# One rule more for issuing the mixer's steps, and a new operand layout for RWKV7's chunk products, in a three-layer forward pass

## The chip, the core and the metric

The program runs on 1 core of one Trainium2 chip: TensorE (PE in the rows, PEld its weight loads), VectorE (DVE), ScalarE (ACT), GpSimd (POOL), and SyncE (SP), whose queue starts the DMAs. The metric is device microseconds per execution. Before the change three runs took 3031.47, 3031.53 and 3036.08 us, median 3031.53. One further execution was profiled; the rows below come from it.

## What is computed

512 tokens of width 2048 pass through three layers and a final norm, in float32: an attention layer with decaying scores ("fox"), a sliding-window attention layer ("swa"), and a mixer of two linear recurrences side by side ("mix"). Each layer multiplies by a large input matrix and a large output matrix. What the change touches is the RWKV7 half of the mixer: 16 heads of width 64, each with a recurrence over tokens.

```python
def _rwkv7_scan(r, w, k, v, a_vec, b_vec):
    def step(S, inp):
        r_t, w_t, k_t, v_t, a_t, b_t = inp
        sa = jnp.einsum('bhij,bhj->bhi', S, a_t)
        S = S * w_t[:, :, None, :] + sa[..., None] * b_t[:, :, None, :] + v_t[..., None] * k_t[:, :, None, :]
        return S, jnp.einsum('bhij,bhj->bhi', S, r_t)
...
o_rwkv, v_first = _rwkv7_branch(rw, v_first, ...)
o_hgrn = _hgrn2_branch(hg, lower_bounds[l], g_norm_w[l])
y = jnp.einsum('btc,cd->btd', jnp.concatenate([o_rwkv, o_hgrn], axis=-1), w_out[l])
h = _layer_norm(ALPHA * h + y, ln_w[l], ln_b[l])
```

The kernel computes the scan in 4 chunks of 128 tokens. Within a chunk it needs, per head, the 128 x 128 products of the decayed vectors (a, r) with (b, k), then the inverse of a triangular matrix built from them, then a short chain that carries the state from chunk to chunk.

## The kernel before

**The stream.** All large products go through `stream`. Weights come in chunks of 128 x 512 (`raw`), are split into a high part (`wh`, ScalarE) and a low part (`wl`, GpSimd), and each slot of the stream issues three TensorE products of 512 columns (high x high, high x low, low x high; `mm3`) into a PSUM tile `proj`. In the rows these are `proj<-hh,wh`, `proj<-hl,wh` and `proj<-hh,wl`; here they are called stream products. There are 10272 of them in the program.

**The steps.** All other work is written as threads: lists of steps, each a Python function that issues a few instructions on several engines. Before each slot `stream` calls `side`, which goes through the threads and issues every step that `ready` lets through, within a budget. `ready` decides by a planner's clock (`Clock`, `Engine.cost`): a step may go once the step before it in its thread is finished by that clock (plus a margin) and the events it needs are past. `require` and `drain` issue steps whether they are ready or not. TensorE runs its instructions in the order in which they were issued, so a step issued too early makes the stream products behind it wait too.

**PSUM.** A step that multiplies takes a PSUM tile from a pool: `s` and `t` have 2 buffers each, `y` 1, `proj` 3. A new tile can be written only when the one that had the buffer before has been read out by DVE or ACT. The planner's clock knows of this (`tile` notes when the old tile is free, and `note` lets the engine wait for it), but `ready` does not ask for it.

**RWKV7.** Eight units (pairs of heads) follow each other; unit `u` has the threads prep, M, K and B of `rwkv_unit`. The steps the prediction speaks of, with the tile names that the rows show:

- `p_lora`: products `s<-wdh,uph` and three like it into both `s` tiles, read out by ACT into `sgt` and `ez`. `p_kk2`: head sums `t<-pm,ones_r`, `t<-pr,ones_r`, read out by DVE (`pm<-t`). `p_tok`: four transposes, `t<-ident,bk` or `t<-ident,ev`, read out by ACT (`tokb`, `tokk`, `tokv`).
- `m_split`, `m_split2` and `m_step`, four times per unit (once per chunk): the operands `bk` and `ar` are split into high and low parts (`bkhl`, `arhl`), then `s<-arhl,bkhl` products into both `s` tiles, one per head, read out by four DVE operations (`kt`, `yh`). `m_zo`: `t<-tokv,kt`, read out by ACT (`zo`).
- `inv_8` and `inv_16`: many short DVE operations on `ly` that invert small blocks. `lev16` to `lev32b`, the level steps: 112 very small products (`t<-td,yh`, `t<-wd,ly`, `t<-ly,wd`).
- `ch_z`, `ch_u`, `ch_u2`, `ch_u3`, `ch_s`, `ch_o`: the chain over chunks. `ch_z` is `t<-sbd,ar`, read out by DVE into `chz`; `ch_u` and `ch_u3` are `t<-chz,wd` (or `t<-zo,wd`), read out by DVE into `chu`. `f_1` to `f_3`: group norm, DVE operations on `gn`, then transposes `t<-ident,zo`.

The other half, HGRN2, has eight units of its own (`hgrn_unit`) with tiles from the same two pools, and follows while the stream goes on. Nearly all instructions are recorded at one line (L175, a helper), so rows are told apart by tile names.

Of the kernel before, what the change touches and what calls it, by code (L numbers as in the profile page):

```python
# [6 lines left out]
F32 = mybir.dt.float32  # L7
# [22 lines left out]
class Clock:  # L30
# [7 lines left out]
    def __init__(self):  # L38
        self.t = dict.fromkeys(("tensor", "vector", "scalar", "gpsimd", "sync"), 0.0)
        self.w, self.r, self.free, self.dead = {}, {}, {}, set()  # L40
        self.fin = 0.0
        self.aset = None
        self.mode = None

        self.port = {"vector": [], "gpsimd": []}
# [11 lines left out]
    def note(self, eng, cost, outs, ins, lat=0.0, mode=None, shared=False):  # L57
# [27 lines left out]
            del p[:-24]  # L85
        self.t[eng] = t + cost
        fin = t + cost + lat
        for c, kind in use.items():
            d = self.w if kind else self.r
            if d.get(c, (0.0, eng))[0] <= fin:  # L90
                d[c] = (fin, eng)
        self.fin = max(self.fin, fin)

    def last(self, name):

        return max([v[0] for d in (self.w, self.r) for k, v in d.items() if k[0] == name] + [0.0])


def isap(x):
# [89 lines left out]
class Timed:  # L189
    def __init__(self, clock, nc):  # L190
        for n in ("tensor", "vector", "scalar", "gpsimd", "sync"):
            setattr(self, n, Engine(clock, getattr(nc, n), n))


class Kern:
# [109 lines left out]
    def set(self, ev):  # L305
        self.ev[ev] = self.clock.fin
# [29 lines left out]

    def ready(self, th):
        return th["steps"] and th["ready"] <= self.clk and all(
            self.ev.get(e, 1e9) <= self.clk for e in th["steps"][0][1])

    def side(self):
        t0 = self.clk
# [916 lines left out]
    def rwkv_unit(self, st, u):  # L1259
# [142 lines left out]
        def m_split(c):  # L1402
            def f():
                if c == 0:
                    S["zo"] = P("zo", (128, 4, 2, 128), bufs=2)
                bk = S["bk"][:, c]
                S["bkh", c] = x = P("bkhl", (128, 2, 2, 128), F32R, 2)
                S["arh", c] = y = P("arhl", (128, 3, 2, 128), F32R, 2)
                for h in range(2):
                    nc.scalar.activation(x[own[h], h], bk[own[h]], AF.Copy)  # L1410
                nc.scalar.activation(y[:, 2], S["ar"][:, c], AF.Copy)
            return f

        def m_split2(c):
            def f():
                ar, bk, x, y = S["ar"][:, c], S["bk"][:, c], S["bkh", c], S["arh", c]
                for h in range(2):
                    a, b = own[h], own[1 - h]
                    nc.scalar.activation(y[b, h], ar[a], AF.Copy)
                    nc.vector.tensor_tensor(out=x[b, h], in0=bk[a], in1=x[a, h].bitcast(F32),  # L1420
                                            op=ALU.subtract)
                    nc.vector.tensor_tensor(out=y[a, h], in0=ar[a], in1=y[a, 2].bitcast(F32),
                                            op=ALU.subtract)
            return f

        def m_step(c):
            def f():
                p = [ps("s", (128, 2, 256)) for h in range(2)]  # L1430
                x = S["bkh", c]
                y = [S["arh", c][:, i].rearrange("p a t -> p (a t)") for i in range(3)]
                for i in range(2):
                    for h in range(2):
                        mm(p[h][:, i, :], x[own[h], h, i, :], y[2][own[h], :], i == 0, False,
                           skip_group_check=True)
                for h in range(2):
                    for i in range(2):
                        mm(p[h][:, i, :], x[:, h, i, :], y[h], False, i == 1, skip_group_check=True)
                for h in range(2):  # L1440
                    nc.vector.copy_predicated(out=kt[:, h, :], mask=self.mmask, data=p[h][:, 1, :])
                    nc.vector.copy_predicated(out=mat[:, 2 * c + h, :], mask=self.mmask,
# [900 lines left out]
```

## Time and profile before

| | before |
|---|---|
| three runs | 3031.47, 3031.53, 3036.08 us; median 3031.53 |
| profiled execution | 3026.69 us, of which span 3024.9 us, mean granted clock 0.985 |
| PE busy | 2942.7 us, 97% of the span, 17904 matmuls |
| PEld busy | 2356.2 us, 78% |
| DVE busy | 1560.2 us, 52%, 3481 instructions |
| ACT busy | 1302.4 us, 43%, 2571 instructions |
| POOL busy | 1351.4 us, 45%, 1105 instructions |

In the rows, PEclk is the share of TensorE's clock that was granted: 1.00 is its upper level of 2.4 GHz, a moment at 0.50 its lower one of 1.2 GHz, and a value between them is a mean over a stretch. A matmul's duration includes its way through the array, so matmuls overlap: the distance between two starts is what one costs. "Idle before" is time in which an engine did nothing, and the name behind it is what ended that.

### The profile page before, as it was taken

Reading aid. Unit: us, or ns where it says so; the run is one execution under the profiler, and the core shown is the slowest. Engines: PE = TensorE matmul, PEld = TensorE weight load, DVE = VectorE, ACT = ScalarE, POOL = GpSimd, SP = SyncE. Lnnn points to the kernel's source line nnn. Section 1 sums busy time; section 2 is a strip of 40 time slices with the busy share of each in tenths; the row PEclk is TensorE's granted clock in tenths of the full one; section 3 lists DMA queues with packets and bytes.
Section 4 is the critical chain, followed back from the end, with each engine's and each line's share of the span. In section 5 each row is a group of like instructions: output and inputs, shape, how many; then the busy total and the mean of one; then the engine's idle time right before and its main releaser. Section 6 shows DMA issues by size and latency. Waiting matters only on the chain. (4 is left out here: it accounts for less than half of the span.)

```text
span 3024.9 us, 47964 instructions
## 1 busy us (share of the span) xinstructions
PE 2942.7 (97%) x17904; PEld 2356.2 (78%) x17904; DVE 1560.2 (52%) x3481; ACT 1302.4 (43%) x2571; POOL 1351.4 (45%) x1105
## 2 busy tenths in 40 slices
PE   8999999999999999999999999999999999999996
PEld 5788888888888888888888876677677787888785
DVE  6433333343431235555531277767777766766436
ACT  6444444444433344444443364444444445545233
POOL 3444444444446543444445652223333344444575
PEclk9999999999999999999999999999989999999998
DMA  4333333333335432222234422222222222222343
GB/s 139 108 87 88 94 91 88 94 91 89 93 91 161 140 94 77 75 79 79 76 121 145 123 81 71 62 65 62 64 69 66 76 68 73 81 77 77 103 120 107
DMA packets 192088, 275.79 MB, mean 91 GB/s; under 512 B 50576, under 2 KB 65872, under 8 KB 191856
## 3 DMA queue, kind: packets, MB, share of 16 engines
q1 hardware_dynamic: 191856, 272.73, 31.6%
q8 instruction: 141, 2.31, 0.3%
q14 instruction: 91, 0.75, 0.1%
HBM read 254.51 MB, written 18.16 MB: 90 GB/s over the span
## 5 line engine op out<-in xcount | busy, mean ns | idle before, releaser
L175 POOL TENSOR_TENSOR wl<-raw,wh 128x512 fp32r<-128x512 f32 x847 | 1123.2, 1328 | 1606.8 <-ACT wh L175 1552.6
L175 PE MATMUL proj<-hh,wh 128*128 128x512 f32 x2624 | 1073.2, 409 | 7.1 <-ACT hh L175 5.9
L175 PE MATMUL proj<-hl,wh 128*128 128x512 f32 x2624 | 1036.7, 395 | 4.5 <-DVE hl L175 4.4
L175 PE MATMUL proj<-hh,wl 128*128 128x512 f32 x2624 | 1037.2, 395 | 3.2 <-POOL wl L175 3.1
L175 ACT ACTIVATE wh<-raw 128x512 fp32r<-128x512 f32 x848 | 530.7, 627 | 822.0 <-PE proj L175 587.1
L175 PEld LDWEIGHTS proj<-hh,wh 128*128 128x128 f32 x2624 | 498.8, 190 | 116.1 <-issue 10.6
L175 PEld LDWEIGHTS proj<-hh,wl 128*128 128x128 f32 x2624 | 499.1, 190 | 114.7 <-POOL wl L175 6.5
L175 PEld LDWEIGHTS proj<-hl,wh 128*128 128x128 f32 x2624 | 500.1, 191 | 95.7 <-DVE hl L175 8.0
L175 PE MATMUL proj<-yh,wh 128*128 128x512 f32 (+1 forms) x640 | 249.8, 390 | 0.0
L175 PE MATMUL proj<-yh,wl 128*128 128x512 f32 (+1 forms) x640 | 248.2, 388 | 0.7 <-POOL wl L175 0.4
L175 ACT ACTIVATE t<-t,sm 128x257 f32<-128x257 f32 (+5 forms) x256 | 133.0, 521 | 257.2 <-DVE sm L175 197.3
L175 PE MATMUL proj<-yl,wh 128*128 128x512 f32 (+1 forms) x632 | 240.9, 388 | 0.0
L175 PEld LDWEIGHTS proj<-yh,wl 128*128 128x128 f32 x640 | 120.2, 188 | 26.8 <-POOL wl L175 2.4
L175 DVE TENSOR_TENSOR pt<-proj,t 128x512 f32<-128x512 f32 x32 | 22.1, 691 | 229.1 <-PE proj L175 116.5
L175 PEld LDWEIGHTS proj<-yh,wh 128*128 128x128 f32 x640 | 120.3, 188 | 24.4 <-issue 0.9
L175 PEld LDWEIGHTS proj<-yl,wh 128*128 128x128 f32 x632 | 118.8, 188 | 23.9 <-issue 0.2
L175 DVE TENSOR_TENSOR qf<-proj,rsb 128x512 f32<-128x512 f32 x48 | 33.2, 691 | 154.5 <-PE proj L175 154.2
L175 DVE TENSOR_SCALAR t<-t,sm 128x256 f32<-128x256 f32 (+3 forms) x256 | 101.7, 418 | 6.7
L175 DVE COPY pt<-t 128x384 f32<-128x384 f32 (+1 forms) x96 | 51.2, 534 | 99.8 <-PE t L175 99.8
L175 DVE RECIPROCAL sm<-sm 128x1 f32<-128x1 f32 (+1 forms) x192 | 31.4, 164 | 117.4 <-ACT t L175 115.8
L175 PE MATMUL t<-ident,t 128*128 128x128 f32 x544 | 90.5, 272 | 0.0
L175 DVE CUSTOM_DVE_ANT_0 t<-s,c 128x128 f32<-128x128 f32 (+2 forms) x128 | 49.9, 390 | 71.6 <-PE s L175 71.6
(412 smaller groups left out, 3752.4 us busy)
## 6 DMA issues: line engine op xcount, KB each, us to landing
raw<-in_w_mix_dram SPq DMA_DIRECT2D x260, 256.0 KB, 3.0
raw<-in_w_fox_dram SPq DMA_DIRECT2D x256, 256.0 KB, 3.0
raw<-in_w_swa_dram SPq DMA_DIRECT2D x144, 256.0 KB, 3.0
raw<-in_w_foxo_dram SPq DMA_DIRECT2D x64, 256.0 KB, 3.2
raw<-in_w_swao_dram SPq DMA_DIRECT2D x64, 256.0 KB, 3.1
raw<-in_w_mixo_dram SPq DMA_DIRECT2D x64, 256.0 KB, 3.1
c<-cd SPq DMA_DIRECT2D x32, 256.0 KB, 3.7
xd<-pt SPq DMA_DIRECT2D x32, 256.0 KB, 2.4
```

The lines of the kernel that those rows point to most:

```text
L175: r = f(*a, **k)
```

## The change

Two things. First, `ready` also asks a new function, `banks`: it looks up which PSUM tiles the step will take (table `BANKS`), takes the buffers of that pool in turn, oldest first, and lets the step through only when the planner's clock has passed the time at which the last user of each is done. This holds for RWKV7's and HGRN2's steps that take `s` or `t` tiles; not for those that take `y`, and not for steps issued by `require` or `drain`. `last` is rewritten to keep its answer in a dictionary; its value is the same.

Second, `m_split`, `m_split2` and `m_step` keep both heads of a unit in the 128 rows of one operand: rows 0 to 63 are one head, rows 64 to 127 the other, with the high part in one place and the low part in another. ACT makes both high parts in two operations of 128 x 256 (before: four of 64 x 256 and one of 128 x 256), DVE both low parts in two of 128 x 256 (before: four of 64 x 256), and TensorE makes twelve products over 64 rows (before: four over 64 rows and four over 128 rows, in which high and low part lay under each other).

```diff
+BANKS = dict(p_lora="ss", m_step="ss", lev64="s", lev_m="s", **dict.fromkeys(
+    ("p_kk2", "p_bonus", "p_tok", "m_zo", "lev16", "lev16b", "lev32", "lev32b", "ch_z", "ch_u",
+     "ch_u2", "ch_u3", "ch_s", "f_3", "tok", "state", "fin3"), "t"))
...
     def ready(self, th):
         return th["steps"] and th["ready"] <= self.clk and all(
-            self.ev.get(e, 1e9) <= self.clk for e in th["steps"][0][1])
+            self.ev.get(e, 1e9) <= self.clk for e in th["steps"][0][1]) and self.banks(
+                th["steps"][0][0]) <= self.clk
+
+    def banks(self, f):
+
+        name = [n for n in f.__qualname__.split(".") if n not in ("<locals>", "f")][-1]
+        t = 0.0
+        for i, p in enumerate(BANKS.get(name, "")):
+            pool, bufs = self.psum[p]
+            q = self.slots.get((id(pool), p), [])
+            if i >= bufs - len(q):
+                t = max(t, self.clock.last(q[i - (bufs - len(q))]) + self.clock.HOP)
+        return t
...
-                bk = S["bk"][:, c]
-                S["bkh", c] = x = P("bkhl", (128, 2, 2, 128), F32R, 2)
-                S["arh", c] = y = P("arhl", (128, 3, 2, 128), F32R, 2)
-                for h in range(2):
-                    nc.scalar.activation(x[own[h], h], bk[own[h]], AF.Copy)
-                nc.scalar.activation(y[:, 2], S["ar"][:, c], AF.Copy)
+                S["x", c] = x = P("bkhl", (128, 2, 2, 128), F32R, 2)
+                S["y", c] = y = P("arhl", (128, 2, 2, 128), F32R, 2)
+                nc.scalar.activation(x[:, 0], S["bk"][:, c], AF.Copy)
+                nc.scalar.activation(y[:, 0], S["ar"][:, c], AF.Copy)
...
-                ar, bk, x, y = S["ar"][:, c], S["bk"][:, c], S["bkh", c], S["arh", c]
-                for h in range(2):
-                    a, b = own[h], own[1 - h]
-                    nc.scalar.activation(y[b, h], ar[a], AF.Copy)
-                    nc.vector.tensor_tensor(out=x[b, h], in0=bk[a], in1=x[a, h].bitcast(F32),
+                for t, hl in ((S["bk"], S["x", c]), (S["ar"], S["y", c])):
+                    nc.vector.tensor_tensor(out=hl[:, 1], in0=t[:, c], in1=hl[:, 0].bitcast(F32),
                                             op=ALU.subtract)
-                    nc.vector.tensor_tensor(out=y[a, h], in0=ar[a], in1=y[a, 2].bitcast(F32),
-                                            op=ALU.subtract)
...
                 p = [ps("s", (128, 2, 256)) for h in range(2)]
-                x = S["bkh", c]
-                y = [S["arh", c][:, i].rearrange("p a t -> p (a t)") for i in range(3)]
-                for i in range(2):
-                    for h in range(2):
-                        mm(p[h][:, i, :], x[own[h], h, i, :], y[2][own[h], :], i == 0, False,
-                           skip_group_check=True)
-                for h in range(2):
+                x = S["x", c]
+                y = S["y", c].rearrange("p n a t -> p n (a t)")
+                for n, (a, b) in enumerate(((0, 0), (0, 1), (1, 0))):
                     for i in range(2):
-                        mm(p[h][:, i, :], x[:, h, i, :], y[h], False, i == 1, skip_group_check=True)
+                        for h in range(2):
+                            mm(p[h][:, i, :], x[own[h], a, i, :], y[own[h], b, :],
+                               n == i == 0, n == 2 and i == 1, skip_group_check=True)
```

Up to unit 1's `p_lora` the order of TensorE's instructions is the same in both programs. From there on the rule moves steps against the stream. Three places, on PE; in the changed program the same helper line is L178, because lines were added above it.

First, where unit 3's preparation meets unit 2's chain. Before, the head sums, the second set of transposes and the chain's `t<-chz,wd` follow each other:

```order
L175 MATMUL y<-chu,yh_15303 64x64 x4
L175 MATMUL t<-ident,bk 128x128 x4
L175 MATMUL proj<-hh_95,wh 128x512
L175 MATMUL proj<-hl_108,wh 128x512
L175 MATMUL proj<-hh_95,wl 128x512
L175 MATMUL t<-sbd_15307,ar_17196 128x128
L175 MATMUL t<-pm,ones_r 128x512
L175 MATMUL t<-pr,ones_r 128x512
L175 MATMUL t<-ident,bk 128x128 x4
L175 MATMUL t<-chz,wd 64x64 x2
L175 MATMUL proj<-hh_95,wh 128x512
```

After, at the same point of the same two units:

```order
L178 MATMUL y<-chu,yh_15303 64x64 x4
L178 MATMUL t<-ident,bk 128x128 x4
L178 MATMUL proj<-hh_95,wh 128x512
L178 MATMUL proj<-hl_108,wh 128x512
L178 MATMUL proj<-hh_95,wl 128x512
L178 MATMUL t<-sbd_15307,ar_17243 128x128
L178 MATMUL t<-ident,ev 128x128 x4
L178 MATMUL proj<-hh_95,wh 128x512
L178 MATMUL proj<-hl_109,wh 128x512
L178 MATMUL proj<-hh_95,wl 128x512
L178 MATMUL proj<-hh_96,wh 128x512
L178 MATMUL proj<-hl_110,wh 128x512
```

After six stream products there, `t<-chz,wd` and the second transposes follow; the head sums stand 57 stream products ahead of the first of these rows.

Second, unit 1's `p_lora` (`s<-wdh,uph` and the three products behind it) and unit 0's first `m_step` (`s<-arhl,bkhl`), which takes the same two buffers. Before:

```order
L175 MATMUL s<-wdl,upl 128x512
L175 MATMUL proj<-hh_92,wh 128x512
L175 MATMUL proj<-hl_103,wh 128x512
L175 MATMUL proj<-hh_92,wl 128x512
L175 MATMUL s<-arhl,bkhl 128x256 x8
```

After:

```order
L178 MATMUL s<-wdl,upl 128x512
L178 MATMUL proj<-hh_92,wh 128x512
L178 MATMUL proj<-hl_102,wh 128x512
L178 MATMUL proj<-hh_92,wl 128x512
L178 MATMUL proj<-hh_92,wh 128x512
L178 MATMUL proj<-hl_103,wh 128x512
L178 MATMUL proj<-hh_92,wl 128x512
L178 MATMUL t<-pq,ones_r 128x512
L178 MATMUL t<-pt,ones_r 128x512
L178 MATMUL proj<-hh_93,wh 128x512
L178 MATMUL proj<-hl_104,wh 128x512
L178 MATMUL proj<-hh_93,wl 128x512
```

Three more stream products stand behind these and then the `m_step`: 12 stream products between the two steps where there were 3.

Third, the last two level steps of unit 3 (`t<-td,yh` of 32 rows, then `t<-wd,ly`). Before:

```order
L175 MATMUL t<-td,yh_15304 32x32 x16
L175 MATMUL proj<-hh_97,wh 128x512
L175 MATMUL proj<-hl_113,wh 128x512
L175 MATMUL proj<-hh_97,wl 128x512
L175 MATMUL proj<-hh_90,wh 128x512
L175 MATMUL proj<-hl_98,wh 128x512
L175 MATMUL proj<-hh_90,wl 128x512
L175 MATMUL t<-wd,ly 32x32 x16
```

After:

```order
L178 MATMUL t<-td,yh_15304 32x32 x16
L178 MATMUL s<-arhl,bkhl 128x256 x12
L178 MATMUL proj<-hh_95,wh 128x512
L178 MATMUL proj<-hl_108,wh 128x512
L178 MATMUL proj<-hh_95,wl 128x512
L178 MATMUL t<-wd,ly 32x32 x16
```

Here the steps moved together: 3 stream products and an `m_step` between them, where there were 6 stream products.

## Rows read from the trace of the kernel before

**Rows 1.** Stretches: us, busy (instructions) by engine, PEclk, DMA share, GB/s.

```profile
1770.00:2440.00 670.00, 630.63 (x5384) 478.33 (x5383) 505.78 (x1084) 293.81 (x575) 214.67 (x165) 0.95 0.26 67
```

**Rows 2.** Waits of PE from 1770 to 2440 us: total, times, longest.

```profile
PE t L175 <- DVE pm L175: 11.1, 4, 2.8
PE t L175 <- DVE chz L175: 5.1, 5, 1.0
PE t L175 <- DVE em L175: 4.2, 2, 2.1
PE t L175 <- ACT tokk L175: 3.7, 1, 3.7
PE t L175 <- ACT zo L175: 2.9, 6, 0.5
...
PE s L175 <- ACT sgt L175: 2.1, 1, 2.1
PE s L175 <- DVE yh L175: 1.8, 2, 0.9
```

**Rows 3.** Timeline of PE, 2039 to 2044 us: start, duration, instruction, idle before.

```profile
2039.39 0.50 PE L175 MATMUL t<-pm,ones_r 128*128 128x512 f32 x1
...
2040.01 0.66 PE L175 MATMUL t<-ident,bk 128*128 128x128 f32 x4
2043.43 0.69 PE L175 MATMUL t<-chz,wd 64*64 64x64 f32 x4 [2.77 <-DVE pm L175]
```

**Rows 4.** Timeline of DVE in the same stretch.

```profile
2039.87 0.16 DVE L175 TENSOR_TENSOR invt<-ly 64x14 f32<-64x14 f32 x1
...
2042.70 0.67 DVE L175 TENSOR_SCALAR pm<-t 128x512 f32<-128x512 f32 x1
```

**Rows 5.** Timeline of DVE, 2014 to 2018 us.

```profile
2016.26 1.42 DVE L175 TENSOR_TENSOR arhl<-ar,arhl 64x256 fp32r<-64x256 f32 x1
2017.71 0.29 DVE L175 TENSOR_TENSOR chz<-t,zo 128x128 f32<-128x128 f32 x1
```

**Rows 6.** Short stretches around waits and level steps.

```profile
1851.00:1862.00 11.00, 10.52 (x139) 8.27 (x136) 2.65 (x9) 4.91 (x11) 1.27 (x1) 0.53 0.05 15
1916.00:1920.00 4.00, 4.00 (x23) 2.86 (x18) 3.28 (x7) 2.19 (x5) 1.28 (x1) 0.57 0.23 66
1964.00:1975.00 11.00, 10.27 (x31) 7.49 (x32) 7.93 (x16) 3.06 (x7) 4.48 (x3) 0.53 0.08 25
...
2042.00:2054.00 12.00, 10.57 (x33) 7.59 (x34) 8.80 (x20) 3.09 (x5) 1.63 (x2) 0.57 0.08 22
2125.00:2136.00 11.00, 10.27 (x54) 7.94 (x56) 9.08 (x18) 3.15 (x6) 2.53 (x2) 1.00 0.10 26
...
2210.00:2217.00 7.00, 6.51 (x22) 4.41 (x23) 4.14 (x8) 2.47 (x4) 1.28 (x1) 0.51 0.13 37
...
2298.00:2306.00 8.00, 8.00 (x27) 5.65 (x26) 6.77 (x12) 2.14 (x4) 1.37 (x1) 0.57 0.14 35
```

**Rows 7.** Timeline of PE: one m_step of chunk products and what follows.

```profile
1790.79 1.18 PE L175 MATMUL s<-arhl,bkhl 64*128 64x256 f32 x8
1791.81 0.40 PE L175 MATMUL proj<-hh,wh 128*128 128x512 f32 x1
```

**Rows 8.** Timeline of PE in parts of that m_step.

```profile
1790.79 0.39 PE L175 MATMUL s<-arhl,bkhl 64*128 64x256 f32 x2
...
1791.23 0.74 PE L175 MATMUL s<-arhl,bkhl 128*128 128x256 f32 x4
```

**Rows 9.** Timeline of PEld at its first two products.

```profile
1790.79 0.19 PEld L175 LDWEIGHTS s<-arhl,bkhl 64*128 64x128 f32 x2 [0.24 <-issue]
```

**Rows 10.** Splits on DVE and ACT, 1770 to 2440 us: busy, mean ns, idle before.

```profile
L175 DVE TENSOR_TENSOR bkhl<-bk,bkhl 64x256 fp32r<-64x256 f32 x64 | 37.3, 582 | 1.6
...
L175 ACT ACTIVATE arhl<-ar 64x256 fp32r<-64x256 f32 x64 | 26.6, 416 | 1.4
L175 ACT ACTIVATE arhl<-ar 128x256 fp32r<-128x256 f32 x32 | 13.4, 418 | 6.6 <-DVE ar L175 6.0
```

More of the change, by code (lines that the diff above doesn't have):

```diff
@@ L40, in __init__ @@
         self.w, self.r, self.free, self.dead = {}, {}, {}, set()
+        self.used = {}
         self.fin = 0.0
@@ L87, in note @@
         fin = t + cost + lat
+        for name in {c[0] for c in use}:
+            self.used[name] = max(fin, self.used.get(name, 0.0))
         for c, kind in use.items():
@@ L94, in last @@
     def last(self, name):
-        return max([v[0] for d in (self.w, self.r) for k, v in d.items() if k[0] == name] + [0.0])
+        return self.used.get(name, 0.0)
 def isap(x):
```

## Prediction

> **What bounds the kernel now.** TensorE: its busy time is 97% of the span, and the number of stream products is fixed, so time can be won only where TensorE stands still or runs at its lower clock. I first cut the span into stretches. From 1770 to 2440 us, where RWKV7's eight units run, TensorE is busy 630.6 of 670.0 us and the granted clock is 0.95 [rows 1]: 39.4 us of standing still, and 5% of 670, some 33 us, lost to the clock. DVE comes next with 505.8 us. Then the waits of TensorE in that stretch [rows 2]. The reader is to see two kinds among them. In one kind the name behind the wait is an operation that only reads a PSUM tile out, of a step that has nothing to do with the waiting one: `pm` (11.1 us in 4 waits), `tokk` (3.7), `zo` (2.9 in 6), `sgt` (2.1), `yh` (1.8 in 2). These are waits for space. In the other kind the waiting product needs what is being made: `chz`, `em`.
>
> The timeline shows how a wait for space comes about. `t<-chz,wd` stands still for 2.77 us [rows 3]. The head sum that began at 2039.39 could be read out soon after 2040, but DVE has a row of short inversion operations in front, from 2039.87 on, and gets to `pm<-t` at 2042.70 [rows 4]. With two `t` buffers, the second product behind it must wait, and the stream products behind that one wait too, though they need nothing from it.
>
> Last, short stretches around such waits [rows 6]. The granted clock is 0.53, 0.57, 0.51 and 0.57 in four stretches that begin with a wait for space (1964, 2042, 2210, 2298), and 1.00 behind another wait of the same length (2125). A value between 0.5 and 1 is a mean of the two levels. What was lost is the missing share times the length: 11 x 0.47, 12 x 0.43, 7 x 0.49 and 8 x 0.43, that is 5.2 + 5.2 + 3.4 + 3.4 = 17.2 us. Two other low stretches, 0.53 at 1851 and 0.57 at 1916, have no long wait ahead of them but the level steps, very small products; they lose 5.2 and 1.7 us.
>
> **The change part by part.**
>
> *The rule for space.* It removes no instruction. Where a step would have found its buffer in use, stream products go first. At the 2.77 us wait, the head sums now stand far ahead and six stream products come before `t<-chz,wd`; between `p_lora` and the first `m_step` (the `sgt` wait) stand 12 stream products instead of 3. The waits for space sum to 11.1 + 3.7 + 2.9 + 2.1 + 1.8 = 21.6 us [rows 2]: term (a), −21.6. With them go the low-clock stretches behind four of them: term (b), −17.2 [rows 6].
>
> What comes in their place: the planner's clock is not the chip's, and a step may still meet a full buffer. I counted, in the order of the instructions, how often a `t` tile follows the last user of its buffer with no stream product between: 26 times before, 14 after. Priced at the shortest wait for space, 2.9 / 6 = 0.48 us [rows 2], the 14 cost 6.7 us: term (c), +6.7. Its bounds are 0 (the other products between them cover it, as for many of the 26 now) and 14 x 1.0 = 14 us.
>
> The rule also moves steps of the chain, and with it the level steps come closer together in units 2, 3, 4, 5 and 7, as in the third place shown. Since level steps alone pull the clock down, I charge each of these five units with the smaller loss seen, 1.7 us [rows 6]: term (d), +8.6. Its bounds: 0, and 5 x 5.2 = 26.
>
> Does the chain get later as a whole? Unit 2's last transposes stand 75 stream products later than before, but the last unit's 15 earlier, and HGRN2's last ones 12 earlier. So the output products that need the mixer's results wait for nothing new: 0, and the stream products cover the delay in the middle.
>
> On SP and POOL the weight loads and `wl` operations move by a place or two against the mixer's own; both engines have room (POOL 214.7 of 670 us) [rows 1], so 0.
>
> *The splits.* Per chunk ACT makes 2 operations instead of 5, DVE 2 instead of 4. An operation of 128 x 256 takes ACT as long as one of 64 x 256 (418 against 416 ns) [rows 10], so the halves are saved whole: 32 x 3 x 0.42 = 40 us of ACT and, at 582 ns, 64 x 0.58 = 37 us of DVE. Neither engine sets the end, so this counts only where TensorE waits for them. One such place recurs: the `chz` wait, 1.0 us five times. There DVE is still at the fourth subtraction (1.42 us at 2016.26) when `chz` could be made, which starts at 2017.71 [rows 5]. With two subtractions instead of four, at least 0.84 us of each 1.03 goes: term (e), −4.2. Bounds 0 and −5.1. For the other DVE waits, `em` above all, I count nothing: they come from short operations of the group norm that do not change.
>
> *The products.* An `m_step` costs 1.02 us from its first start to the next stream product [rows 7]. Of that the four full-height products take 1791.81 − 1791.23 = 0.58, 0.145 each, and the two pairs of half-height ones 1791.23 − 1790.79 = 0.44, 0.22 each [rows 7, 8]. Four pairs now stand for the four full-height products. If a pair went on costing 0.22, that is 4 x 0.075 x 32 = +9.6 us; if the 0.44 holds 0.15 us of changing the array over that is now paid only once, −4.8 us. I take 0: the two products of a pair start together, and so do their two weight loads [rows 8, 9], so a pair in a row of pairs should cost what a full-height product of as many columns costs, and there are six such places before and after.
>
> The Trainium skill ("TensorE: Matmul & The Clock Gate", section on LDWEIGHTS) says that a weight load takes its time by columns, whatever the number of rows. Taken alone that speaks against twelve loads for eight: four more at half of 0.22 us, 32 times, is an estimate of +14 us. The row shows two loads within one load's 0.19 us, so the rule holds for one load and adds nothing for a pair; by the row the sum is 0.
>
> *Sum.* −21.6 − 17.2 + 6.7 + 8.6 − 4.2 = −27.7 us. The profiled execution took 3026.7 us, so 2999.0; the median of the three runs is 4.8 us above that execution, so I predict 3031.5 − 27.7 = 3003.8, that is 3004 us.
>
> **The rivals.**
>
> *The waits come back under another name.* If DVE is what is late, and not the space, then a step held back for its buffer finds its operand late instead. For it: DVE is busy 75% of the stretch, and a subtraction of 0.42 us can take 1.42. Against: in the 2.77 us wait nothing was missing but the space. Half of (a) and (b) stays: −10.8 − 8.6 + 6.7 + 8.6 − 4.2 = −8.3, 3023 us.
>
> *The rule asks for the wrong buffer.* It takes the buffers in turn. But in the `tokk` wait, the product waits for the read-out of the tile written directly before it, so the program does not always hand them out in turn. Then `tokk` and `zo` waits (6.6 us) and the clock loss at 1964 (5.2) stay: −15.9, 3016 us.
>
> *Slower: the level steps pull the clock down in every unit.* Place: the four level steps, now closer, with half-height products between them. Price: the 5.2 us of unit 0 [rows 6] in all eight units is 41.6, against the some 16 that the stretch now loses beside the 17.2. With these 25 more, and with the 17.2 not won back because the clock is low there anyway, the balance is −21.6 − 4.2 + 6.7 + 25.3 = +6.2, 3038 us. It decides from some 19 us of new loss on, four units that fall as unit 0 did. Against it: with level steps in all eight units the stretch as a whole still has 0.95 [rows 1], so most of them run without such a fall now.
>
> **How the numbers follow.** The forecast gets 0.58, the returning waits 0.20, the wrong buffer 0.10, the level steps 0.12. About 0.2% (6 us) is what a measurement of this kernel can tell from no change. Faster by more than that are the forecast, the wrong buffer and part of the returning waits: 0.76. Within it the rest of these: 0.13. Slower: 0.11. The range: at the low end all waits for space, the clock behind them and (e) to its bound, nothing of (c) and (d), −43.9, and the −4.8 of the products: 2983. At the high end the returning waits with little left of them: 3030. The forecast's own range is 2985 to 3018.
>
> **What would show it.** Right: `pm`, `tokk`, `sgt` and `yh` all but gone from TensorE's waits, standing still in that stretch near 20 us, granted clock 0.97 or more, `chz` waits under 0.3 us, and 12 half-height products from first start to next stream product in about 1.0 us. An `m_step` of 1.3 us would show the products mispriced. New waits of 1 us or more for DVE operands would show the first rival; low clock in stretches without waits the third. It is wrong as a whole if TensorE's idle time in the stretch stays above 35 us.

## The result and the profile after

The changed kernel takes 2994.2 us (median of four runs, 2986.3 to 2998.5) against 3032.4 us of the kernel before on the same chip: a ratio of 0.9869, 95% interval [0.9846, 0.9891], or some 38 us less. Run again beside other kernels it gave 0.9878 [0.9864, 0.9891]. The prediction was 3004 us; the direction and the place are as predicted, and the gain is some 10 us larger than its sum.

The profiled execution took 2993.78 us, span 2992.0 us. Its busy times, from the page of the profile:

```profile
PE 2926.8 (98%) x18032; PEld 2349.3 (79%) x18032; DVE 1518.8 (51%) x3417; ACT 1256.3 (42%) x2473; POOL 1353.5 (45%) x1105
```

128 matmuls more (four for each of 32 `m_step`), and 98 ACT and 64 DVE instructions fewer. Then the stretch of RWKV7's units (busy time and instructions by engine, granted clock, DMA share, GB/s), to be held against [rows 1]:

```profile
1770.00:2440.00 670.00, 648.74 (x5703) 499.84 (x5702) 490.53 (x1074) 268.15 (x515) 231.74 (x177) 0.96 0.26 71
```

TensorE stands still for 670.0 − 648.7 = 21.3 us there, where it was 39.4. Its waits in that stretch, to be held against [rows 2]:

```profile
PE t L178 <- DVE chz L178: 6.3, 5, 2.4
PE proj L178 <- ACT wh L178: 3.7, 2, 3.4
PE t L178 <- DVE chu L178: 3.3, 3, 1.6
PE proj L178 <- POOL wl L178: 2.8, 5, 1.1
PE t L178 <- DVE zo L178: 2.5, 4, 1.0
PE t L178 <- DVE ly L178: 0.9, 2, 0.7
PE y L178 <- DVE chu L178: 0.8, 3, 0.4
PE t L178 <- DVE sbd L178: 0.3, 1, 0.3
PE t L178 <- ACT zo L178: 0.2, 1, 0.2
```

`pm`, `tokk`, `sgt` and `yh` are gone, and the wait for ACT's `zo` fell from 2.9 to 0.2 us: of 21.6 us of waits for space, 0.2 is left. (Two waits before that [rows 2] does not show, one for `sbd` of 1.0 us and one for `ez` of 0.2, were for space too; with them it is 22.8.) What remains is waits for data; `chz` did not fall (5.1 before, 6.3 now), and waits for split weights (`wh`, `wl`) and for `chu` are new or longer.

A fixed window holds more work in the faster kernel. For comparisons I therefore take the same work in every kernel: from the 6584th stream product to the 8250th. Its time is divided into standing still (the sum of TensorE's gaps), clock (half of each moment at 0.50, the most that a moment at 1.2 instead of 2.4 GHz can lose), and the rest, one profiled execution each:

| us | whole | still | clock | rest |
|---|---|---|---|---|
| before | 698.8 | 39.4 | 35.8 | 623.5 |
| changed | 664.3 | 21.3 | 25.6 | 617.5 |
| changed, a second execution (e10) | 658.2 | 21.8 | 15.4 | 621.1 |
| rule alone (e1) | 675.3 | 24.1 | 22.2 | 629.1 |
| products and splits alone (e2) | 682.6 | 32.6 | 30.7 | 619.3 |
| changed, splits in halves (e9) | 671.1 | 21.9 | 25.6 | 623.6 |
| changed, `bk` on DVE (e13) | 674.2 | 24.7 | 34.1 | 615.4 |
| changed, level hold 2.4 us (e5) | 648.9 | 17.5 | 8.5 | 622.9 |
| changed, level hold 3.6 us (e11) | 647.0 | 16.1 | 8.5 | 622.4 |
| before, level hold 2.4 us (e12) | 700.8 | 40.3 | 32.4 | 628.1 |

Outside this stretch the changed kernel and the one before differ by under 1.5 us in each of three other stretches. Two executions of the very same changed program stand still alike (21.3 and 21.8 us) and differ by 10 us in the clock, so a single profile tells standing still well and the clock only roughly.

Half of each such moment is too much: a stream product that costs 0.23 us at the upper level costs 0.43 at the lower one, which is a little under half lost, and while TensorE stands still there is nothing to lose. Two of them at the lower level, in the kernel before:

```profile
1970.45 0.63 PE L175 MATMUL proj<-hl,wh 128*128 128x512 f32 x1
1970.88 0.63 PE L175 MATMUL proj<-hh,wl 128*128 128x512 f32 x1
```

What the table takes too much for the clock is missing in its rest, so rests at different clocks are not to be compared. So I price the low moments in a second way: each pair of neighbouring products at its mean distance between starts at the upper level, over all 14 profiles, and what a low moment takes beyond that is its loss. Before, this gives 29.8 us of clock and 629.5 us of work at full clock (what is left beside standing still and clock); in the two executions of the change 20.9 and 13.7 us of clock, but 622.1 and 622.7 us of work. The same program so has the same work, as it should, and the change makes the work some 7 us shorter.

### The profile page after: what moved, and what is told of

Read it like the earlier page. It is cut to its first block, busy times and chain, and to the rows that moved or that the text cites. A ratio compares the mean times of both kernels' runs of the same rounds, so it can differ in the third digit from the quotient of the medians.

```text
span 2992.0 us, 48037 instructions
## 1 busy us (share of the span) xinstructions
PE 2926.8 (98%) x18032; PEld 2349.3 (79%) x18032; DVE 1518.8 (51%) x3417; ACT 1256.3 (42%) x2473; POOL 1353.5 (45%) x1105
## 4 chain that ended last, share of the span: by engine, by line
PE 89%; DVE 6%; issue 2%; DMA 1%; POOL 1%; ACT 1%; SPq 0%; POOLq 0%; DVEq 0%; ACTq 0%
PE proj L178 72%; PE t L178 7%; PE s L178 6%; PE y L178 3%; DVE invt L178 1%; DVE hh L178 1%; POOL wl L178 1%; DVE gn L178 1%; DVE ly L178 1%; DMA raw<-in_w_fox_dram 0%; DVE zo L178 0%; DVE hn L178 0%; SPq L178 0%; DMA yf<-in_x_dram 0%; DVE raw L178 0%
## 5 line engine op out<-in xcount | busy, mean ns | idle before, releaser
L178 POOL TENSOR_TENSOR wl<-raw,wh 128x512 fp32r<-128x512 f32 x847 | 1123.7, 1329 | 1575.4 <-ACT wh L178 1492.9
L178 PE MATMUL proj<-hh,wh 128*128 128x512 f32 x2624 | 1069.7, 408 | 11.0 <-ACT hh L178 6.7
L178 PE MATMUL proj<-hh,wl 128*128 128x512 f32 x2624 | 1034.1, 394 | 3.9 <-POOL wl L178 3.9
L178 PE MATMUL proj<-hl,wh 128*128 128x512 f32 x2624 | 1033.7, 394 | 3.4 <-DVE hl L178 3.3
L178 ACT ACTIVATE wh<-raw 128x512 fp32r<-128x512 f32 x848 | 530.5, 627 | 827.8 <-PE proj L178 603.8
L178 PEld LDWEIGHTS proj<-hh,wh 128*128 128x128 f32 x2624 | 496.8, 189 | 121.8 <-issue 9.6
L178 PEld LDWEIGHTS proj<-hh,wl 128*128 128x128 f32 x2624 | 496.9, 189 | 115.1 <-POOL wl L178 7.9
L178 PEld LDWEIGHTS proj<-hl,wh 128*128 128x128 f32 x2624 | 497.7, 190 | 94.8 <-DVE hl L178 6.7
L178 PE MATMUL proj<-yh,wh 128*128 128x512 f32 (+1 forms) x640 | 249.5, 390 | 0.0
L178 PE MATMUL proj<-yh,wl 128*128 128x512 f32 (+1 forms) x640 | 248.0, 388 | 0.3
L178 ACT ACTIVATE t<-t,sm 128x257 f32<-128x257 f32 (+5 forms) x256 | 133.1, 521 | 257.0 <-DVE sm L178 197.0
L178 PE MATMUL proj<-yl,wh 128*128 128x512 f32 (+1 forms) x632 | 240.9, 388 | 0.0
L178 PEld LDWEIGHTS proj<-yh,wl 128*128 128x128 f32 x640 | 120.2, 188 | 26.0 <-POOL wl L178 1.6
L178 PEld LDWEIGHTS proj<-yh,wh 128*128 128x128 f32 x640 | 120.2, 188 | 24.6 <-issue 0.9
L178 DVE TENSOR_TENSOR pt<-proj,t 128x512 f32<-128x512 f32 x32 | 22.1, 691 | 229.0 <-PE proj L178 97.2
L178 PEld LDWEIGHTS proj<-yl,wh 128*128 128x128 f32 x632 | 118.7, 188 | 24.1 <-issue 0.2
L178 DVE TENSOR_TENSOR qf<-proj,rsb 128x512 f32<-128x512 f32 x48 | 33.2, 691 | 154.4 <-PE proj L178 154.2
L178 DVE TENSOR_SCALAR t<-t,sm 128x256 f32<-128x256 f32 (+3 forms) x256 | 101.5, 417 | 6.7
L178 DVE COPY pt<-t 128x384 f32<-128x384 f32 (+1 forms) x96 | 51.3, 534 | 99.8 <-PE t L178 99.8
L178 DVE RECIPROCAL sm<-sm 128x1 f32<-128x1 f32 (+1 forms) x192 | 31.4, 163 | 117.4 <-ACT t L178 115.8
L178 PE MATMUL t<-ident,t 128*128 128x128 f32 x544 | 90.4, 272 | 0.0
L178 DVE CUSTOM_DVE_ANT_0 t<-s,c 128x128 f32<-128x128 f32 (+2 forms) x128 | 49.9, 390 | 71.9 <-PE s L178 71.9
```

The lines of the kernel that those rows point to most:

```text
L178: r = f(*a, **k)
```

## The experiments

Three batches, each on one chip with the kernel before beside it (medians 3030.07, 3031.21 and 3029.45 us).

**The two halves alone.** e1 is the changed kernel with the old `m_split`, `m_split2` and `m_step`. e2 is the changed kernel without the rule:

```diff
-            self.ev.get(e, 1e9) <= self.clk for e in th["steps"][0][1]) and self.banks(
-                th["steps"][0][0]) <= self.clk
+            self.ev.get(e, 1e9) <= self.clk for e in th["steps"][0][1])
```

> The rule for space alone, with the old splits and products. Theory A (the time came from waits for space and the clock behind them): the waits named pm, tokk, sgt and yh are gone, standing still in the RWKV7 stretch falls from 39 to some 22 us, and at least 20 of the 38 us come, a time of 2998 to 3010 us. Theory B (the lighter splits carry the gain, the rule only shuffles): within 6 us of the kernel before, about 3027 to 3035 us.

> The new splits and products alone, without the rule. Theory A: waits for space named pm or tokk remain (20 immediate reuses of a t buffer are left of 26, against 14 with the rule), standing still stays above 30 us, and the gain is under 12 us: 3020 to 3032 us. Theory B: most of the 38 us, 2995 to 3008 us. An m_step followed by stream products costs 0.90 us to the next start plus 0.10 us on the one after, 1.01 in all, as much as before.

e1: 3013.52 us, 0.9946 [0.9930, 0.9961]. e2: 3010.78 us, 0.9945 [0.9933, 0.9957]. Each half is worth some 17 us, and the two together nearly give what the whole gives (33 of 37 to 38 us). Neither came as theory A had it: e1 gave less than the 20 us that it asks for, e2 more than its 12, so splits and products carry about as much as the rule. TensorE's waits of e1 from 1770 to 2440 us, the first two and those for space:

```profile
PE t L178 <- DVE zo L178: 4.9, 8, 1.9
PE t L178 <- DVE chu L178: 3.6, 5, 1.4
...
PE t L178 <- ACT zo L178: 1.4, 3, 0.5
...
PE t L178 <- DVE pm L178: 0.5, 2, 0.2
```

The rule alone removes the waits for space but for 1.9 us. Of e2 the same view:

```profile
PE proj L178 <- ACT wh L178: 7.5, 4, 4.1
PE t L178 <- DVE zo L178: 7.3, 3, 3.5
...
PE s L178 <- ACT sgt L178: 2.2, 1, 2.2
```

Without the rule the `sgt` wait of [rows 2] stays, as it should; `pm` and `tokk` are gone here too, since shorter ACT and DVE work moves the steps in the planner's order, and other waits have come. In all, 2.8 us of waits for space are left in e2. So e2's 17 us are not the price of the products: only 4.2 of 16.2 us in the table stand in its rest (4.6 by the second way), 6.8 in standing still and 5.1 in the clock.

**Is the gain a lucky order?** `MARGIN`, the planner's margin behind a step, moves every step a little. Without and with the change:

```diff
-    NRAW, NW, LEAD, LEAD_RAW, BUDGET, MARGIN, POOL_LO = 3, 3, 2, 2, 1.8, 0.1, True
+    NRAW, NW, LEAD, LEAD_RAW, BUDGET, MARGIN, POOL_LO = 3, 3, 2, 2, 1.8, 0.15, True
```

> The kernel before with one number of the planner changed, its margin of 0.10 us made 0.15, which has nothing to do with PSUM: another order of the same work. Theory A: waits for space remain, 23 immediate reuses instead of 26, time within 12 us of before, 3020 to 3040 us. Theory C (any other order would have gained, the old one happened to be a bad one): 2995 to 3010 us.

> The changed kernel with the planner's margin 0.15 instead of 0.10. To be held against the same margin without the change, which took 3042 us (1.0038 of the kernel before). If the change gains by what it does, it gains at this margin too, by some 30 to 45 us: 2997 to 3012 us. If its gain at margin 0.10 was a lucky order, this lands anywhere from 3010 to 3045 us.

> The kernel before with margin 0.05, a third order of the old work. 24 immediate reuses of a t buffer (26 before). If orders without the rule all stand still for some 40 us, 3020 to 3045 us. If the old order was a bad one, 2995 to 3015 us.

> The changed kernel with margin 0.05, the pair of the run before. By what the change does: 30 to 45 us under that run. By luck: any sign. In this order the program hands out the buffer just used six times in a row (once in the changed kernel, seven times before), so if the rule asks for the wrong buffer there, some zo or tokk waits of 0.5 us return.

| margin | without the change | with it |
|---|---|---|
| 0.05 | 0.9998 [0.9989, 1.0007] | 0.9927 [0.9912, 0.9942] |
| 0.10 | 1 | 0.9878 [0.9864, 0.9891] |
| 0.15 | 1.0038 [1.0024, 1.0051] | 0.9886 [0.9872, 0.9901] |

At all three margins the change gains: 22, 37 and 46 us, at 0.05 less than the 30 to 45 that I expected. The order alone is worth up to some 15 us either way; the direction does not hang on it, the size does.

Two things in these profiles narrow the account. First, the waits for space hang on the order too. Counted as waits for an operation that reads out an `s` or `t` tile and whose result the waiting product does not use, there are 3.1 us at margin 0.05 and 9.1 at 0.15 without the rule, where the kernel before has 22.8; and margin 0.05 is still no faster than the kernel before (10 us shorter in the stretch of the table, 13 us longer behind it). What the rule lowers in every order is standing still as a whole: at the three margins from 31.1, 39.4 and 44.7 us to 23.8, 21.3 and 21.0 with the change, and in all nine profiles with the rule it is 16 to 25 us, in all five without it 31 to 45. Why waits for data also shrink with the rule is not shown. Second, the clock does not always follow: at margin 0.05 the table's way gives 30.7 us lost without the change and 34.1 with it.

In e8 (margin 0.05 with the change) the waits for `zo` came back, as was expected there if the rule asks for the wrong buffer:

```profile
PE t L178 <- ACT zo L178: 2.4, 5, 0.5
```

Four of the five, 1.9 us, are waits for space. Whether the wrong buffer or a wrong time on the planner's clock lets them through, no run tells.

**The splits.** e9 is the changed kernel with each split in two operations of 64 rows, the products unchanged:

```diff
-                nc.scalar.activation(x[:, 0], S["bk"][:, c], AF.Copy)
-                nc.scalar.activation(y[:, 0], S["ar"][:, c], AF.Copy)
+                for h in own:
+                    nc.scalar.activation(x[h, 0], S["bk"][h, c], AF.Copy)
+                    nc.scalar.activation(y[h, 0], S["ar"][h, c], AF.Copy)
...
-                    nc.vector.tensor_tensor(out=hl[:, 1], in0=t[:, c], in1=hl[:, 0].bitcast(F32),
-                                            op=ALU.subtract)
+                    for h in own:
+                        nc.vector.tensor_tensor(out=hl[h, 1], in0=t[h, c],
+                                                in1=hl[h, 0].bitcast(F32), op=ALU.subtract)
```

> The changed kernel, but the splits are made in halves of 64 rows: 4 operations on ACT instead of 2 and 4 on DVE instead of 2 per chunk, with the new products and the rule kept. If the new products gain by fewer changes of the array's division alone, the time stays within 6 us of the changed kernel, 2988 to 3000 us, and what TensorE works at full clock stays at 617 us in the RWKV7 stretch. If the lighter splits carry the part that was not foreseen, the time goes up by 8 to 16 us, to 3002 to 3010 us, with standing still and lower clock making up the difference.

3001.56 us, 0.9908 [0.9891, 0.9924], some 9 us above the changed kernel run elsewhere (0.9878), with intervals that touch. Its waits for `chz`:

```profile
PE t L178 <- DVE chz L178: 10.2, 7, 1.8
```

3.9 us more for `chz`, yet 21.9 us of standing still in all against 21.3: others fell by nearly as much. What the table shows lies in its rest, 2.5 to 6 us above that of the two executions of the changed kernel (6 us above both, 628.8 us of work, by the second way). That shorter splits shorten TensorE's waits is not shown.

**What the `chz` waits are.** e13 is the changed kernel with two GpSimd operations of each unit's preparation on DVE:

```diff
-            nc.gpsimd.tensor_tensor(out=bk[:, :, 0, :], in0=c4(kq), in1=c4(a), op=ALU.mult)
-            nc.gpsimd.tensor_tensor(out=bk[:, :, 0, :], in0=bk[:, :, 0, :], in1=S["Pi"], op=ALU.mult)
+            nc.vector.tensor_tensor(out=bk[:, :, 0, :], in0=c4(kq), in1=c4(a), op=ALU.mult)
+            nc.vector.tensor_tensor(out=bk[:, :, 0, :], in0=bk[:, :, 0, :], in1=S["Pi"], op=ALU.mult)
```

The reason stands in the changed kernel's timeline. The longest `chz` wait, on PE (start, duration, instruction, idle before):

```profile
2187.10 0.39 PE L178 MATMUL proj<-hh,wl 128*128 128x512 f32 x1
2189.89 0.41 PE L178 MATMUL t<-chz,wd 64*64 64x64 f32 x4 [2.40 <-DVE chz L178]
```

DVE just before, where the inversion's operations stand ahead of `chz`:

```profile
2183.98 1.23 DVE L178 TENSOR_TENSOR ly<-ly,invt 64x24 f32<-64x24 f32 x1
2185.24 0.18 DVE L178 TENSOR_TENSOR invt<-ly 64x30 f32<-64x30 f32 x1
2185.46 1.19 DVE L178 TENSOR_TENSOR ly<-ly,invt 64x30 f32<-64x30 f32 x1
2186.69 1.26 DVE L178 TENSOR_TENSOR invt<-ly 64x32 f32<-64x32 f32 x1
2187.98 0.18 DVE L178 TENSOR_TENSOR ly<-ly,invt 64x32 f32<-64x32 f32 x1
...
2189.44 0.29 DVE L178 TENSOR_TENSOR chz<-t,chz 64x128 f32<-64x128 f32 x1
```

And GpSimd:

```profile
2183.86 1.32 POOL L178 TENSOR_TENSOR bk<-pq,ez 128x512 f32<-128x512 f32 x1 [1.21 <-PE t L178]
2185.25 1.36 POOL L178 TENSOR_TENSOR bk<-bk,pt 128x512 f32<-128x512 f32 x1
2186.63 1.28 POOL L178 TENSOR_TENSOR wl<-raw,wh 128x512 fp32r<-128x512 f32 x1
```

The same kind of operation takes 0.18 us, and 1.2 us when a GpSimd operation is under way at its start; the slow ones end at 2185.21, 2186.65 and 2187.95, 0.03 to 0.04 us after GpSimd's ends at 2185.18, 2186.61 and 2187.91. Three such stalls of 1.0 us make up more than the wait.

> The changed kernel, with the two products of 128 x 512 that make bk in the preparation of each RWKV7 unit on VectorE instead of GpSimd. VectorE gets some 16 us more work. Theory (the waits for chz that the change left come from VectorE operations of two SBUF operands that stand still while GpSimd's bk operations run): the chz waits from 1770 to 2440 us fall from 6.3 us to 3 or less. Rival (they come from the length of VectorE's queue): chz stays at 6 us or grows. Its order has only 3 stream products between the first two level steps in units 0, 2, 4 and 7, so the clock loses 25 us or more either way, and the time is 2985 to 3005 us.

3002.48 us, 0.9909 [0.9895, 0.9923]. TensorE's waits:

```profile
PE proj L178 <- POOL wl L178: 6.1, 6, 2.6
PE proj L178 <- ACT wh L178: 4.8, 3, 3.3
...
PE t L178 <- DVE chz L178: 2.5, 3, 1.0
```

`chz` fell from 6.3 to 2.5 us as the theory had it, and the three left again stand behind DVE operations of 1.1 to 1.7 us that ran beside GpSimd's. The order changed as well, so the cause is supported by this run and shown by the timeline, not isolated. The kernel is slower: other waits took the place, and the clock lost 34.1 us, mostly in the places that the next part is about.

**The level steps and the clock.** Stretches around the first two level steps of units 0, 2, 4, 5, 6 and 7 in the changed kernel; in the order, 3 stream products stand between the two in units 0, 2, 5 and 7, and 6 and 12 in units 4 and 6:

```profile
1846.00:1858.00 12.00, 12.00 (x175) 9.53 (x173) 5.92 (x14) 6.06 (x12) 1.28 (x1) 0.72 0.08 26
1998.00:2010.00 12.00, 12.00 (x156) 9.29 (x156) 6.65 (x16) 4.79 (x9) 1.26 (x1) 0.58 0.15 42
2138.00:2148.00 10.00, 9.91 (x184) 8.18 (x183) 8.41 (x13) 3.92 (x9) 2.53 (x2) 1.00 0.16 50
2213.00:2224.00 11.00, 11.00 (x167) 8.88 (x164) 5.32 (x13) 5.89 (x12) 1.26 (x1) 0.69 0.14 43
2288.00:2298.00 10.00, 9.36 (x153) 7.40 (x151) 7.26 (x12) 2.47 (x6) 5.86 (x5) 1.00 0.26 77
2363.00:2377.00 14.00, 14.00 (x185) 11.18 (x184) 4.68 (x14) 3.49 (x8) 4.96 (x7) 0.58 0.18 53
```

TensorE is busy without a gap in the four that fall, and at half of each low moment 0.72, 0.58, 0.69 and 0.58 mean 3.4 + 5.0 + 3.4 + 5.9 = 17.7 us lost. e5 and e11 hold the second level step back on the planner's clock, so that 6 to 15 (2.4 us) or 9 to 15 (3.6 us) stream products come between:

```diff
     def banks(self, f):
...
-        t = 0.0
+        t = self.hold if name == "lev16b" else 0.0
...
             nc.vector.tensor_scalar_mul(y16, p[:, :, 0:16], self.rm[:, 1:2])
+            self.hold = self.clk + 2.4
```

> The changed kernel, and lev16b is held back until 2.4 us of the planner's clock after lev16, so that 6 to 15 stream products stand between these two level steps where there were 3 in four of eight units. In the changed kernel's trace the clock fell for 6.8, 10.2, 6.8 and 13.7 us in exactly the four units with 3 products between them. Theory D (these two steps close together pull the clock down): the falls at level steps shrink from 37.5 us to under 14, that is some 12 us less, 2978 to 2986 us. Theory E (the clock falls by any low work of TensorE in the stretch, and where the two stand does not decide): falls of about the same sum elsewhere, 2990 to 3000 us.

> The changed kernel once more, on the same chip as the three below, for a narrower interval. Expected: 2990 to 2997 us, ratio 0.987 to 0.989 (four runs so far: 2986 to 2999).

> The changed kernel, with the second level step held back 3.6 us of the planner's clock behind the first, where the earlier kernel with this hold took 2.4 us. In the order, 9 to 15 stream products now stand between the two in every unit (2.4 us: 6 to 15; the change: 3 in four units). Theory (level steps close together pull the clock down): clock losses from 1770 to 2440 us at or under the 10.2 us that 2.4 us left, below 12 in any case, 2975 to 2985 us. Rival (the gain of the 2.4 us hold was a lucky order): the losses go back to some 25 us and the time to 2990 to 3000.

e5: 2982.77 us, 0.9852 [0.9837, 0.9867], as expected, though the low moments at the level steps shrank from 37.5 to 17 us and not to under 14. e11: 2976.70 us, 0.9829 [0.9816, 0.9842], beside e10 (the change again) with 2992.42 us, 0.9878 [0.9864, 0.9891] on the same chip; the intervals do not meet, and e11 is the fastest kernel of this study. Of the 11.2 us by which its stretch in the table is shorter than e10's, 5.7 are standing still and 6.9 the clock, with 1.3 more of rest: the hold changes the order, and not the clock alone. The stretch of e11 as a whole, and the first two level steps of its units 0 and 7:

```profile
1770.00:2440.00 670.00, 653.90 (x5815) 503.59 (x5814) 497.05 (x1095) 278.26 (x532) 250.06 (x190) 0.99 0.28 73
...
1849.00:1859.00 10.00, 10.00 (x204) 8.27 (x203) 7.33 (x19) 3.98 (x10) 2.52 (x2) 1.00 0.01 2
...
2351.00:2360.00 9.00, 9.00 (x183) 7.12 (x183) 6.11 (x13) 3.31 (x9) 5.29 (x8) 1.00 0.19 60
```

e10's second execution of the changed program, units 0, 2, 4, 6 and 7:

```profile
1846.00:1858.00 12.00, 12.00 (x206) 9.66 (x203) 6.88 (x15) 6.70 (x13) 1.28 (x1) 0.86 0.11 25
1998.00:2010.00 12.00, 12.00 (x160) 9.07 (x156) 7.77 (x20) 7.18 (x17) 1.44 (x2) 0.86 0.09 23
2138.00:2148.00 10.00, 9.91 (x101) 7.40 (x100) 5.67 (x14) 4.93 (x10) 1.28 (x1) 0.83 0.23 67
...
2288.00:2298.00 10.00, 10.00 (x91) 7.75 (x91) 6.81 (x14) 5.01 (x10) 1.74 (x2) 0.83 0.19 55
2363.00:2377.00 14.00, 14.00 (x166) 10.16 (x162) 7.27 (x20) 4.53 (x11) 4.18 (x6) 0.88 0.14 40
```

The same four units fall for a shorter time, but units 4 and 6, with 6 and 12 products between the steps, fall now as well, and all six lose the same 1.7 us. In this execution the distance does not decide. In e13, where 3 products stand between the two steps in units 0, 2, 4 and 7, just these lose most at their level steps; units 0 and 7:

```profile
1835.00:1848.00 13.00, 12.52 (x129) 9.41 (x127) 4.73 (x12) 3.61 (x9) 0.99 (x1) 0.52 0.02 6
...
2374.00:2389.00 15.00, 15.00 (x171) 11.60 (x168) 4.57 (x11) 3.40 (x9) 3.90 (x7) 0.53 0.17 49
```

Over the five profiles with the change named here (changed, e5, e10, e11, e13) the clock fell at all 12 places with 3 products between the two steps, by 4.0 us on average, and at 10 of 28 with 6 or more, by 0.8 us over the 28 (falls that begin at the two steps or right behind them, half of their length). Over all 14 profiles it is 37 of 38 places with 3 products, 3.8 us on average, and 33 of 74 with 6 or more, 1.2 us. Then the hold without the change, e12:

```diff
-            self.ev.get(e, 1e9) <= self.clk for e in th["steps"][0][1])
+            self.ev.get(e, 1e9) <= self.clk for e in th["steps"][0][1]) and (
+                "lev16b" not in th["steps"][0][0].__qualname__ or self.hold <= self.clk)
```

> The kernel before, with the hold of 2.4 us on the second level step and nothing of the change. 6 to 12 stream products stand between the two level steps in every unit (before: 3 in two units, 9 in the others), and 24 t buffers are still taken with no stream product between (before: 26). Theory: the waits for space stay near 20 us, with the clock losses behind them; only the 13.6 us that the clock lost in units 0 and 2 go: 3012 to 3022 us. If the hold gives 0 to 3 us here, level steps are not what pulled the clock down in those units; if it gives over 25, the waits for space were not worth what the prediction says.

3026.31 us, 0.9988 [0.9979, 0.9997]: 3 to 4 us, not the 7 to 17 that I expected. Two stretches of e12 at the level steps of units 0 and 3, with 6 and 9 products between:

```profile
1851.00:1864.00 13.00, 13.00 (x201) 10.27 (x197) 5.89 (x14) 5.36 (x12) 1.50 (x1) 0.74 0.08 21
...
2086.00:2100.00 14.00, 14.00 (x217) 11.51 (x217) 10.85 (x24) 7.82 (x16) 4.18 (x3) 0.71 0.30 87
```

The clock falls here in spite of the distance, and so it does at six of e12's eight places. So a short distance of the level steps makes a fall likely and longer, and in the changed kernel a greater one took most of these losses away; in the kernel before it did not, and what else pulls the clock down there stays open.

## Why the prediction was right, and where its terms were off

- **(a), waits for space, −21.6:** right for this order: 21.4 us of them went, and the rule alone removes them (e1: 1.9 left). It is not the only thing that can: 2.8 us are left in e2 and 3.1 at margin 0.05, both without it, though in e2 the `sgt` wait stays. What shows the rule's worth is standing still, 39.4 to 24.1 us in e1.
- **(c), immediate reuses, +6.7:** too high. 14 such reuses cost 0.2 us of waits for space, near the lower bound of 0.
- **The first rival, waits under another name,** took that place in part. The named waits for data grew from 15.9 us (in the same view of the kernel before: `chz` 5.1, `em` 4.2, `pt` 2.4, `wl` 1.6, `sbd` 1.5 without the wait for space, `pr` 0.7, `chu` and `tokv` 0.2 each) to 20.6. Standing still fell by 18.1 us, where (a) + (c) + (e) had −19.1: the sum was right by luck in part, with two terms wrong against each other: (c) was 6.5 us too high, (e) 5.4 too low.
- **(e), `chz` waits, −4.2:** wrong. The step that failed is "there DVE is still at the fourth subtraction". All five waits of 1.0 us stood behind a subtraction of 1.41 to 1.42 us, and its three neighbours take 0.42; in all five the fourth was slow because a GpSimd operation (`wl`) was running when it began. From the timeline of GpSimd in the kernel before:

```profile
2015.98 1.42 POOL L175 TENSOR_TENSOR wl<-raw,wh 128x512 fp32r<-128x512 f32 x1 [4.45 <-ACT wh L175]
```

  It ends at 2017.40, the subtraction of [rows 5] at 2017.68. The extra 1.0 us is the whole wait, and fewer subtractions do not buy it. Those five are gone, but five others came with 6.3 us, four behind operations of the inversion and one behind those of a unit's preparation. The two `em` waits, which the prediction put down to short operations that do not change, are of the same kind: the `gn` operations in front of them took 1.1 to 1.2 us beside GpSimd's and 0.17 without.
- **(b) and (d), the clock, −17.2 + 8.6 = −8.6:** right in direction, too small: by the table −10.2 in one execution of the changed program, −20.4 in another (−8.9 and −16.1 by the second way). The granted clock of the stretch is 0.96 in the one and 0.98 in the other, where 0.97 was named. Sorted by what stands ahead of a fall, the table's 35.8 us before are 17.1 behind waits for space, 8.5 behind waits for data (`pt`, and `em` twice) and 10.2 at the first two level steps; in the two executions of the change they are 0, 5.1 and 20.5, and 0, 5.1 and 10.2. So (b) was right in size. (d) came out as +10.3 in the one and 0 in the other: of its five units 2, 5 and 7 fell in the first, 3 and 4 did not, and 2 had fallen before. Not priced at all was what the waits for data gave back, 3.4 us.
- **The third rival, the level steps,** was right as a mechanism and wrong as a balance: they cost some 18 us in the four units that fall in that profile of the changed kernel, but the new loss is 10.3 us there and none in the second execution, far from the 19 us at which it was to decide. And the losses behind the waits for space went, which this rival had staying. e11 shows that most of what the level steps cost can be had back.
- **The second rival, the wrong buffer:** not at this margin, where `tokk` is gone and ACT's `zo` is 0.2 us. At margin 0.05 waits for `zo` came back, with 1.9 us for space and no `tokk`, so it was not refuted as a mechanism, but it is cheap.
- **The products, 0 between −4.8 and +9.6:** right for an `m_step` by itself. PE in the changed kernel, against [rows 7]:

```profile
1786.95 0.98 PE L178 MATMUL s<-arhl,bkhl 64*128 64x256 f32 x12
1787.86 0.50 PE L178 MATMUL proj<-hh,wh 128*128 128x512 f32 x1
1788.20 0.40 PE L178 MATMUL proj<-hl,wh 128*128 128x512 f32 x1
1788.43 0.39 PE L178 MATMUL proj<-hh,wl 128*128 128x512 f32 x1
```

  From its first start to the next stream product 0.91 us, where it was 1.02; but the next one then costs 1788.20 − 1787.86 = 0.34 us instead of 0.23. With both it is 1.01, as before, for 20 of the 32. For ten that are followed by another small product the cost is 0.91, where it was 1.26 in the four such cases before. Over all 32 that is about −2 us, an estimate from the medians of these groups. The Trainium skill ("TensorEngine Tiling (Array Packing)", section Key Properties) says that changing the tiling mode drains TensorE; the 0.11 us more of the next stream product agrees. That the four more weight loads add their own time, the +14 us that the prediction weighed, does not show: all twelve products and their loads take 0.91 us.
- **The rest of the sum:** 0 was too high. The table's rest fell by 6.0 and 2.4 us in the two executions; by the second way the work is 7.4 and 6.8 us shorter. In e1 it grew by 4.1 us, in e2 it fell by 4.6: so it does not come with the rule alone. The twelve products themselves give some 2 us of it, and having them is not enough for the remainder: e9, which has them, is at 628.8 us, near the 629.5 before. There is a count, not an experiment: from one product to the next TensorE's tile (rows x columns) changes 754 times before, 729 and 733 times in the two executions of the change, 763 in e1, 729 in e2 and 748 in e9, and over all 14 profiles the work goes with that number (correlation 0.93). That orders with fewer changes between small products and stream products are shorter would fit; no run changed that alone, and the cause of the 5 us stays open.

Together, by the second way: still −18.1 and −17.6 against −19.1, clock −8.9 and −16.1 against −8.6, work −7.4 and −6.8 against 0. In the first execution the gain is larger than the sum by the work alone; in the second, work and clock add about as much each.

## What to carry to other kernels

Before a step is issued on an engine that executes in order, ask not only for its operands but for the space that it will write: each wait for space here also stopped stream products that needed nothing from it. When a wait ends on an operation that took three times its usual length, look at what ran beside it before counting its queue. And spread very small products out: here 9 to 15 stream products instead of 3 between two steps of them gave another 0.5% (0.9829 against 0.9878), about half of it in the clock. In the kernel before, with its other waits, the same kind of hold gave next to nothing (0.9988).

## What the runs showed of the hardware

- A DVE operation with two operands in SBUF stands still while a GpSimd operation runs: 0.18 against 1.2 us for 64 x 30, 0.42 against 1.5 for 128 x 256. Operations that read PSUM did not (`kt<-mmask,s` of 128 x 256 in the changed kernel: 439 ns median, 444 where a GpSimd operation ran at their start, 49 and 15 cases). The Trainium skill ("SBUF — State Buffer", section "SBUF: two separate sides") describes a port pair that one of the two holds for a whole instruction, also against DVE operations with two SBUF inputs where the GpSimd operation reads SBUF; these rows agree.
- The granted clock fell to its lower level in stretches in which TensorE was busy all the time, when these were full of very small products, and the same program lost 25.6 us to it by the table in one execution and 15.4 in the next. Four runs of that program differ by 9 to 12 us, which is of this size.
